# Retention in a hybrid encoder layer: the second half's sums of squares in their own stretch, operand splits moved up and down

## The chip, the cores and the metric

The kernel runs on one core of one Trainium2 chip. The core has a matrix engine (TensorE, PE in the profile), VectorE (DVE), ScalarE (ACT), GpSimd (POOL) and a queue engine, SyncE (SP), that issues most of the DMAs. The metric is the device time of one execution in microseconds (us).

## The reference, cut to what matters

One encoder layer over 1024 tokens of width 1024, in float32:

```python
u = x @ w_in                                    # one projection for both groups of heads
y_ret = GroupNorm(ret_fwd + ret_bwd) * gn_gain * silu(gate)   # 8 heads of 64, chunks of 128
y_att = windowed_gqa(aq, ak, av, sink)          # 8 heads of 64, window +-128
mix   = concat(y_ret, y_att) @ w_out
h     = LN1(alpha * x + mix)
f     = (silu(h @ w_ffn_gate) * (h @ w_ffn_up)) @ w_ffn_down \
        + sigmoid(h @ w_ple_gate) * (p @ w_ple_proj)
out   = LN2(alpha * h + f)
```

GroupNorm runs over the 64 elements of a head: mean, then `rsqrt(mean of squares + eps)`. The change concerns where the sums of squares of this GroupNorm are made, and when some weights are prepared that later stages use.

## The kernel before, in words

**Numbers.** Each float32 product is made of three fast matmuls. An operand is split into a rounded part (hi) and a remainder (lo), and hi x hi, hi x lo and lo x hi are added up in PSUM (`mm3`, lines 77 to 79; in the output projection and later `mm3c`, lines 803 to 805). A split is a copy on ScalarE and a subtraction on VectorE.

**Stages.** After the first projections, the retention heads and attention heads are worked through in four pairs (`NPAIR`): pair i has two retention heads and two attention heads. Around them, further projections of `x` (queries, keys, the gates) run as filling: `enqueue` cuts them into 16 steps a tile (three matmuls of 512 columns each step), and `take` runs so many of these steps at a time. One step of the filling is one *tick*. `run(steps, total)` executes a hand-written list; at each `F` in it, it takes its share of `total` ticks. There is a *stretch* of 48 ticks for the retention of pair 0, one each for pairs 1, 2 and 3 (which hold that pair's attention too), and a last `run` of 16 ticks. These I call stretch 0, 1, 2, 3 and the last run.

**In a stretch** the list has, for the retention, `K` (keys turned and decayed), `r.kv`, `Q` (scores), `r.scan`, `Y` (outputs of a half of the tokens), `E` (`evict`: squares of the half, their split into hi and lo, a copy of the half), `M` (`norm`), and for the attention `sco`, `trn`, `val`. Halves are numbered 0 and 1. `M(h)` multiplies the split squares by a matrix of ones (line 498), so the sums stand in PSUM, and VectorE turns them into a row (line 500). The rest is put into `later`, with due times in ticks after `M` (`LAGS = (3, 6, 9, 12, 15)`): `spread` sends the row to a small tile by DMA (line 505), `power` takes the inverse root on GpSimd (line 508), `store` writes it to DRAM (line 511), `fetch` reads it back over all partitions (line 515), `scaled` multiplies the half by it (line 519). Later the gate of the pair multiplies it too (lines 722 to 724).

**Side work.** Weights that the next stages need as split sums are prepared in the same stretches. Each piece is a `put` (lines 602 to 604): ScalarE copies hi, VectorE subtracts, and SP writes both to DRAM; some puts add or subtract two blocks first (lines 638 and 663). `presplit_out(kt, ...)` makes seven such pieces of the output weights (`wod`), `presplit_small(n, ...)` two pieces of the small operands (`ptd` for n 0 and 1, `ped` for n 2 and 3), `presplit_gate()` 28 pieces of the embedding gate's weights (`pgd`), spread over stretches 0 and 1. All have due times in ticks in the list `side`. The buffers of a put: two in turn for the gate; one (`op`) for all puts of stretch 2, and one for all of stretch 3.

**Order.** In these stretches TensorE's order is the order of the program (`manual_schedule(engines={PE})`). A planner orders the other engines by its own costs; `behind` only tells it that an operation comes after the latest projection matmul. Each engine then executes its list in order, with semaphores for what it depends on. At the end `bp.close()` frees the tiles of the stretches, and the output projection (`product`, lines 825 to 839) begins. Its right operands come from `wod` in DRAM through `stream` (line 814), into tiles of two kinds, `w` and `u`, in turn; `u` lies where tiles of the stretches lay. From there SP's own order is the program's as well.

Of the kernel before, what the change touches and what calls it, by code (L numbers as in the profile page):

```python
# [10 lines left out]
F32R = mybir.dt.float32r  # L11
# [5 lines left out]
P = 128  # L17
S = 1024
# [3 lines left out]
HF = 512  # L22
# [20 lines left out]
def layer(tc, xT, xn, w_first, w_mt, w_rv, w_out, w_pg, w_pe, pT, w_gu, w_dn,  # L43
# [53 lines left out]
    def rawt(w):  # L97
        return wp.tile([P, w], F32, tag="raw", bufs=2, name=nm("raw"))
# [34 lines left out]
    def bt(shape, tag, bufs=None, dt=F32):  # L133
        return bpool.tile(list(shape), dt, tag=tag, bufs=bufs, name=nm(tag))
# [15 lines left out]
    with tc.manual_schedule(engines={mybir.EngineType.DVE, mybir.EngineType.SP}):  # L150
        for kt in range(KT):
            r = xraw[kt]
# [128 lines left out]
    later, side, ticks = [], [], [0]  # L281
# [314 lines left out]
    ped = dr.tile([2, 2, P, 2, HF], F32, name="ped")  # L596
    ptd = dr.tile([4, P, 2, HF], F32, name="ptd")
# [3 lines left out]
    def put(x, o, dst):  # L601
        behind(act.activation(o[:, 0, :], x, AF.Copy))
        behind(dve.tensor_tensor(o[:, 1, :], x, o[:, 0, :].bitcast(F32), ALU.subtract))
        sp.dma_start(dst, o.bitcast(F32))

    def presplit_small(n, o, start):

        hold = []

        def load():  # L610
            r = rawt(2 * HF)
            hold.append(r)
            if n < 2:
                for j in range(4):
                    sp.dma_start(r[:, j * 2 * P:(j + 1) * 2 * P], pT[4 * n + j])
            else:
                sp.dma_start(r, w_pe[n - 2])

        def step(j):
            put(hold[0][:, j * HF:(j + 1) * HF], o, ptd[2 * n + j] if n < 2 else ped[n - 2, j])  # L620

        return [(ticks[0] + start + at, f) for at, f in ((0, load), (4, lambda: step(0)), (7.5, lambda: step(1)))]

# [21 lines left out]
    def presplit_gate():  # L645

        first, other = ([a_tile([P, 2, HF], "pre", t) for _ in range(2)] for t in ("A1", "A0"))
        ops = [a_tile([P, 2, HF], "pro", "A1", F32R) for _ in range(2)]
        n = [0]

        def load(k):
            for j in range(2):
                sp.dma_start((other if k == 1 else first)[j], w_pg[j, k])

        def steps(k):
            raw = other if k == 1 else first

            (a11, a21), (a12, a22) = ([raw[j][:, i, :] for i in range(2)] for j in range(2))

            def s(p, x, *sums):  # L660
                def f():
                    for a in sums:
                        behind(dve.tensor_tensor(*a))
                    put(x, ops[n[0] % 2], pgd[p - 1, k])
                    n[0] += 1
                return f

            return [s(1, a11), s(4, a22), s(2, a12), s(5, a22, (a22, a21, a22, ALU.add)),
                    s(7, a21, (a21, a11, a21, ALU.subtract)), s(6, a11, (a11, a22, a11, ALU.subtract)),
                    s(3, a12, (a12, a12, a11, ALU.subtract))]  # L670

        load(0)
        load(1)
        k0, k1, k2, k3 = map(steps, range(4))
        k1[0] = pair_of(k1[0], lambda: load(2))
        k3[0:0] = [lambda: load(3), lambda: None]
        at = [2 + 3.4 * k for k in range(12)] + [55 + 2.5 * k for k in range(2)] + [60 + 2.2 * k for k in range(7)] + \
            [75 + 2.3 * k for k in range(9)]
        return [(ticks[0] + t, f) for t, f in zip(at, k0 + k1 + k2 + k3, strict=True)]

    def pair_of(f, g):
# [58 lines left out]
    with tc.manual_schedule(engines={mybir.EngineType.PE}):  # L740
        enqueue([mtile(0, ev_av), proj_rv(), *project(1), *project(2), *project(3), gate(0), gate(1), gate(2), gate(3)])

        spare.append(bt([P, S], "aq", 3, F32R))
        twin = lambda t: t.rearrange("p (a b) -> p a b", a=2)
        ops = [twin(spare[1]), a_tile([P, 2, HF], "pro", "A0", F32R)]
        side.extend(presplit_out(0, ops, 17.5, 4))
        side.extend(presplit_out(1, ops, 44, 4, spare[:1]))
        a = Attention(0, ytile(1))
        sco, trn, val = (lambda n: (a.scores, n)), (lambda n: (a.turn, n)), (lambda n: (a.values, n))
        run([F, F, sco(0), F, sco(1), F], 16)  # L750
        run([F, (av_turn, 0), (av_turn, 1), F, trn(0), sco(2), F, trn(1), sco(3), F, val(0), val(1), trn(2), sco(4), F,
             trn(3), sco(5), F, val(2), val(3), trn(4), sco(6), F, trn(5), sco(7), F, val(4), val(5), trn(6), (decay_q, 0),
             F, trn(7), (decay_k, 0, 0), F, val(6), val(7), (decay_k, 0, 1), F], 64)
        assert not side and not later
        y0 = ytile(0)
        side.extend(presplit_gate())
        states = state_tile()
        r = Retention(0, y0, states)
        K, M = (lambda q: (r.keys, q)), (lambda q: (r.norm, q))
        Q = lambda q: (r.scores, q)  # L760
        Y, E = (lambda q: (r.out, q)), (lambda q: (r.evict, q))
        run([K(0), F, K(1), F, F, (r.kv,), Q(0), F, (r.scan,), F, F, F, Y(0), E(0), Q(1),
             F, M(0), (decay_q, 1), F, (decay_k, 1, 0), Y(1), E(1), (decay_k, 1, 1), F, F], 48)
        V = []
        for i in range(1, NPAIR):
            assert i == 1 or not side, len(side)
            M1 = M(1)
            r = Retention(i, ytile(2 * i), states)
            a = Attention(i, ytile(2 * i + 1))
            if i == 2:  # L770
                late = [ytile(6), ytile(7)]
                op = twin(late[1].bitcast(F32R))
                side.extend(presplit_out(2, [op], 2, 3.5, late[:1]))
                side.extend(presplit_small(0, op, 30) + presplit_small(1, op, 38))
            elif i == 3:
                op = twin(bt([P, S], "aq", 3, F32R))
                side.extend(presplit_out(3, [op], 4, 3.5, [bt([P, S], "rk", 2)]))
                side.extend(presplit_small(2, op, 32) + presplit_small(3, op, 40))
            G = [(f, i + 1, *x) for f, x in ((decay_q, ()), (decay_k, (0,)), (decay_k, (1,)))] if i + 1 < NPAIR else \
                [(lambda: None,)] * 3  # L780
            run([K(0), M1, F, K(1), sco(0), F, *V, (r.kv,), Q(0), F, sco(1), F, trn(0), sco(2), (r.scan,), F, trn(1),
                 sco(3), F, val(0), val(1), F, trn(2), sco(4), F, trn(3), sco(5), F,
                 Y(0), E(0), val(2), val(3), Q(1), F, G[0], trn(4), sco(6), M(0), F, G[1], trn(5), sco(7), F,
                 G[2], Y(1), val(4), val(5), E(1), F, trn(6), F, trn(7), F], 48)
            V = [val(6), val(7)]
        run([*V, M(1), F, F, F], 16)

    bp.close()

# [1183 lines left out]
```

## Time and profile before

| | us |
|---|---|
| median of 3 runs (lowest, highest) | 1177.18 (1176.48, 1179.31) |
| the profiled execution | 1177.34 |
| its span, first to last instruction | 1174.9 |
| TensorE busy | 1157.9 (99%) |
| VectorE busy | 900.5 (77%) |
| ScalarE busy | 580.6 (49%) |
| GpSimd busy | 120.1 (10%) |

The granted clock of TensorE is 0.998 of full speed over the span. Times in the rows below are microseconds from the start of the span. By TensorE's timeline, stretch 1 runs from 163.9 to 223.2, stretch 2 to 283.9, stretch 3 to 343.5, the last run to 356.2, where the output projection begins. A row of a timeline gives start, duration, engine, line, operation, the tiles written and read (without their numbers), and in brackets the idle time of the engine before it and what ended it. A trailing "q" on an engine's name is its instruction queue, where DMAs are issued. In a row of waits stand the engine and line that waited, what it waited for, total us, times and the longest one.

### The profile page before, as it was taken

To read this page: it belongs to the slowest core of one execution; us is meant where nothing else is said; L and a number is where in the kernel's file an instruction comes from. 1 tells how busy PE (TensorE), PEld (TensorE's weight loads), DVE (VectorE), ACT (ScalarE), POOL (GpSimd) and SP (SyncE) were. 2 spreads that over 40 slices of the span, in tenths; PEclk is the share of its full clock that TensorE was granted. 3 is DMA by queue.
4 is the path that set the end of the run, shared out by engine and by line. 5 is a ranking of instruction groups with operands and counts; after the bars stand their busy time and mean duration, and the time that the engine had idled before them with its cause. 6 is when DMAs were issued, how large, how long until landed. Compare 5 with 4: busy or idle time off the path is not lost.

```text
span 1174.9 us, 17927 instructions
## 1 busy us (share of the span) xinstructions
PE 1157.9 (99%) x6330; PEld 971.8 (83%) x6330; DVE 900.5 (77%) x1746; ACT 580.6 (49%) x1181; POOL 120.1 (10%) x181
## 2 busy tenths in 40 slices
PE   9999999999998999999999999999999999999996
PEld 7888888888886888887888888888888888888885
DVE  4666688777859688947998988888888875774677
ACT  5566348676756266213444434443344445552463
POOL 2001020202010031000000000000000011133232
PEclk9999999999999999999999999999999999999999
DMA  6345666646446945756322322333224289999977
GB/s 251 94 157 206 244 206 229 216 146 209 154 153 227 384 162 186 286 180 214 114 75 101 132 100 82 125 123 112 99 72 135 80 250 340 350 233 204 261 173 215
DMA packets 84377, 213.86 MB, mean 182 GB/s; under 512 B 12224, under 2 KB 17472, under 8 KB 84288
## 3 DMA queue, kind: packets, MB, share of 16 engines
q1 hardware_dynamic: 75648, 195.94, 47.0%
q0 software_dynamic: 8640, 16.78, 8.2%
q8 instruction: 50, 0.82, 0.3%
q14 instruction: 39, 0.32, 0.1%
HBM read 141.32 MB, written 62.16 MB: 173 GB/s over the span
## 4 chain that ended last, share of the span: by engine, by line
PE 81%; DVE 7%; ACT 5%; DMA 4%; issue 2%; SPq 0%; POOL 0%; DVEq 0%; ACTq 0%; POOLq 0%
PE bmm L803 8%; PE bmm L804 7%; PE bmm L805 7%; PE bt L803 6%; PE bt L804 6%; PE bt L805 6%; PE bs L805 4%; PE bs L804 4%; PE bs L803 4%; PE bo L805 3%; PE bo L803 3%; PE bo L804 3%; PE bmm L77 3%; PE bmm L78 3%; PE bmm L79 3%
## 5 line engine op out<-in xcount | busy, mean ns | idle before, releaser
L77 PE MATMUL bmm<-H,w 128*128 128x512 f32 x240 | 96.9, 404 | 0.0
L78 PE MATMUL bmm<-H,w 128*128 128x512 f32 x240 | 94.1, 392 | 0.0
L79 PE MATMUL bmm<-H,w 128*128 128x512 f32 x240 | 93.8, 391 | 0.0
L1388 ACT ACTIVATE ev<-ev 128x512 f32<-128x512 f32 x42 | 26.5, 630 | 104.3 <-DVE ev L1417 92.8
L1562 POOL DMA_DIRECT2D h0b<-in_w_dn x24 | 21.6, 902 | 541.2 <-DVE ev L1368 505.5
L77 PEld LDWEIGHTS bmm<-H,w 128*128 128x128 f32 x240 | 45.1, 188 | 11.2 <-issue 1.2
L79 PEld LDWEIGHTS bmm<-H,w 128*128 128x128 f32 x240 | 45.2, 188 | 10.3
L78 PEld LDWEIGHTS bmm<-H,w 128*128 128x128 f32 x240 | 45.3, 189 | 8.1
L554 ACT ACTIVATE sc<-sc,st 128x385 f32<-128x385 f32 (+1 forms) x64 | 37.2, 584 | 15.6 <-DVE st L552 15.4
L550 DVE CUSTOM_DVE_ANT_0 sc<-cst,bs,skb 128x384 f32<-128x384 f32 (+1 forms) x64 | 34.8, 574 | 9.3 <-PE bs L549 8.6
L1417 DVE TENSOR_TENSOR ev<-ev,bt 128x512 f32<-128x512 f32 x44 | 30.1, 683 | 12.5 <-PE bt L805 12.5
L1368 DVE TENSOR_TENSOR ev<-ev,bs 128x256 f32<-128x256 f32 x63 | 25.6, 418 | 15.5 <-PE bs L805 14.7
L1390 DVE TENSOR_TENSOR ev<-ev 128x512 f32<-128x512 f32 x42 | 29.0, 691 | 10.5 <-ACT ev L1388 9.0
L803 PE MATMUL bmm<-H,u 128*128 128x512 f32 x92 | 36.2, 393 | 0.2 <-ACT ev L1426 0.2
L804 PE MATMUL bmm<-H,u 128*128 128x512 f32 x92 | 36.1, 392 | 0.0
L805 PE MATMUL bmm<-H,u 128*128 128x512 f32 x92 | 35.8, 389 | 0.0
L560 ACT ACTIVATE sc<-sc,st 128x384 f32<-128x384 f32 (+1 forms) x64 | 34.1, 580 | 0.6 <-DVE st L558 0.5
L71 ACT ACTIVATE H<-ln 128x512 fp32r<-128x512 f32 (+1 forms) x34 | 22.7, 676 | 23.0 <-DVE ln L1052 7.2
L545 POOL COPY sc<-skb 128x1 f32<-128x1 f32 x64 | 15.5, 252 | 180.6 <-PE bt L572 141.9
L72 DVE TENSOR_TENSOR w<-raw,w 128x512 fp32r<-128x512 f32 x34 | 23.1, 686 | 13.8 <-ACT w L71 13.7
L803 PE MATMUL bmm<-H,w 128*128 128x512 f32 x84 | 32.9, 392 | 0.0
L804 PE MATMUL bmm<-H,w 128*128 128x512 f32 x84 | 32.9, 392 | 0.0
(800 smaller groups left out, 3897.8 us busy)
## 6 DMA issues: line engine op xcount, KB each, us to landing
ad<-ev SPq DMA_DIRECT2D x33, 512.0 KB, 2.6
pgd<-pro SPq DMA_DIRECT2D x28, 512.0 KB, 2.9
raw<-in_w_gu SPq DMA_DIRECT2D x22, 512.0 KB, 3.6
ln<-in_w_gu SPq DMA_DIRECT2D x22, 512.0 KB, 4.1
raw<-ad SPq DMA_DIRECT2D x40, 256.0 KB, 5.9
ln<-ad SPq DMA_DIRECT2D x37, 256.0 KB, 6.6
H<-in_w_dn SPq DMA_DIRECT2D x33, 256.0 KB, 7.6
wod<-aq SPq DMA_DIRECT2D x15, 512.0 KB, 2.8
```

The source lines that it names most:

```text
L77: pe.matmul(o, lh, rh, start=start, stop=False)
L78: pe.matmul(o, lh, rl, start=False, stop=False)
L79: recent[0] = pe.matmul(o, ll, rh, start=False, stop=stop).ins.name
L550: dve.tensor_tensor_reduce(sc[g][:, :nk], cst[:, tc0:tc0 + nk], b[:, :nk], slope(i, g), skb[:, 2 * i + g:2 * i + g + 1], ALU.add, ALU.max, ...
L554: act.activation(sc[g][:, :nk + 1], sc[g][:, :nk + 1], AF.Exp, bias=st_[:, 1, j, g:g + 1], accum_out=st_[:, 2, j, g:g + 1])
L560: behind(act.activation(sc[g][:, :nk], sc[g][:, :nk], AF.Copy, scale=st_[:, 3, j, g:g + 1]))
L803: pe.matmul(o, lh, rh, start=start, stop=False, skip_group_check=True)
L804: pe.matmul(o, lh, rl, start=False, stop=False, skip_group_check=True)
L805: pe.matmul(o, ll, rh, start=False, stop=stop, skip_group_check=True)
L1388: act.activation(c[:, 0, :], c[:, 0, :], AF.Silu)
L1390: dve.tensor_tensor(c[:, 1, :], c[:, 0, :], c[:, 1, :], ALU.mult)
L1417: dve.tensor_tensor(get(name), ev[left][:, m, :], right, ALU.add)
```

## The change

- `M(1)`, the sums of squares of the second half, moves from the next stretch (after its `K(0)`; for pair 3, the last run) into its own: at the end of stretch 0, and ahead of `trn(7)` in stretches 1 to 3. The due times of its `spread` to `scaled` are counted from there.
- In stretch 3, the gap between the output weights' puts goes from 3.5 to 3.1 ticks, and the small operands start at ticks 27 and 34 in place of 32 and 40. The last of them is loaded into the tile that held a raw output weight (`rkx`), and its first put uses a second buffer, in the other tile of the tag `rk`.
- In stretch 1, the gate's third group of puts starts at tick 65 in place of 60, 1.9 ticks apart in place of 2.2; the fourth at 78.5 in place of 75, 2 apart in place of 2.3. (These ticks count from the start of stretch 0; its last put is due at 94.5 in place of 93.4.)

```diff
-    def presplit_small(n, o, start):
+    def presplit_small(n, o, start, raw=None, other=None):
...
-            r = rawt(2 * HF)
+            r = rawt(2 * HF) if raw is None else raw
...
-            put(hold[0][:, j * HF:(j + 1) * HF], o, ptd[2 * n + j] if n < 2 else ped[n - 2, j])
+            put(hold[0][:, j * HF:(j + 1) * HF], o if j or other is None else other(), ptd[2 * n + j] if n < 2 else ped[n - 2, j])
...
-        at = [2 + 3.4 * k for k in range(12)] + [55 + 2.5 * k for k in range(2)] + [60 + 2.2 * k for k in range(7)] + \
-            [75 + 2.3 * k for k in range(9)]
+        at = [2 + 3.4 * k for k in range(12)] + [55 + 2.5 * k for k in range(2)] + [65 + 1.9 * k for k in range(7)] + \
+            [78.5 + 2 * k for k in range(9)]
...
         run([K(0), F, K(1), F, F, (r.kv,), Q(0), F, (r.scan,), F, F, F, Y(0), E(0), Q(1),
-             F, M(0), (decay_q, 1), F, (decay_k, 1, 0), Y(1), E(1), (decay_k, 1, 1), F, F], 48)
+             F, M(0), (decay_q, 1), F, (decay_k, 1, 0), Y(1), E(1), (decay_k, 1, 1), F, F, M(1)], 48)
...
-            M1 = M(1)
...
-                side.extend(presplit_out(3, [op], 4, 3.5, [bt([P, S], "rk", 2)]))
-                side.extend(presplit_small(2, op, 32) + presplit_small(3, op, 40))
+                rkx = bt([P, S], "rk", 2)
+                side.extend(presplit_out(3, [op], 4, 3.1, [rkx]))
+                side.extend(presplit_small(2, op, 27) + presplit_small(3, op, 34, rkx, lambda: twin(bt([P, S], "rk", 2, F32R))))
...
-            run([K(0), M1, F, K(1), sco(0), F, *V, (r.kv,), Q(0), F, sco(1), F, trn(0), sco(2), (r.scan,), F, trn(1),
+            run([K(0), F, K(1), sco(0), F, *V, (r.kv,), Q(0), F, sco(1), F, trn(0), sco(2), (r.scan,), F, trn(1),
                  sco(3), F, val(0), val(1), F, trn(2), sco(4), F, trn(3), sco(5), F,
                  Y(0), E(0), val(2), val(3), Q(1), F, G[0], trn(4), sco(6), M(0), F, G[1], trn(5), sco(7), F,
-                 G[2], Y(1), val(4), val(5), E(1), F, trn(6), F, trn(7), F], 48)
+                 G[2], Y(1), val(4), val(5), E(1), F, trn(6), F, M(1), trn(7), F], 48)
             V = [val(6), val(7)]
-        run([*V, M(1), F, F, F], 16)
+        run([*V, F, F, F], 16)
```

## The prediction

> **What bounds the kernel now.** I read the page first, then the list of who waited for whom on TensorE, then that engine's timeline where the longest wait stands, and from there the queue that released it.
>
> ```profile
> span 1174.9 us, 17927 instructions
> ...
> PE 1157.9 (99%) x6330; PEld 971.8 (83%) x6330; DVE 900.5 (77%) x1746; ACT 580.6 (49%) x1181; POOL 120.1 (10%) x181
> ```
>
> TensorE (PE) is busy for nearly all of the span. The change adds no matmul and takes none away, so it can only move the time by adding or removing moments in which PE waits. PE's own waits are few:
>
> ```profile
> PE bt L803 <- DMA u<-wod: 3.2, 2, 2.9
> ...
> PE bt L77 <- DVE sg L1098: 0.9, 1, 0.9
> PE bt L572 <- ACT ptr L574: 0.8, 1, 0.8
> PE bt L428 <- DVE pt L411: 0.7, 1, 0.7
> PE bt L572 <- ACT sc L560: 0.4, 1, 0.4
> ```
>
> Columns: total us, times, longest. The first is the largest by far: the output projection's first product waits for operands that were split earlier, written to DRAM (`wod`) and are now fetched. The L77 wait lies far behind the changed code. The other three lie inside the retention and attention stretches that the change rearranges. PE's timeline at the first wait:
>
> ```profile
> 356.22 0.39 PE L803 MATMUL bt<-w,H 128*128 128x512 f32 x1
> ...
> 359.98 0.47 PE L803 MATMUL bt<-u,H 128*128 128x512 f32 x1 [2.92 <-DMA u<-wod]
> ...
> 361.21 0.47 PE L803 MATMUL bt<-w,H 128*128 128x512 f32 x1 [0.30 <-DMA w<-wod]
> ...
> 362.46 0.47 PE L803 MATMUL bt<-u,H 128*128 128x512 f32 x1 [0.31 <-DMA u<-wod]
> ...
> 363.22 0.40 PE L803 MATMUL bt<-w,H 128*128 128x512 f32 x1
> ...
> 365.96 0.39 PE L803 MATMUL bs<-w,H 128*128 128x512 f32 x1
> ```
>
> Each L803 opens a group of three matmuls on one of four operands. The second column of the product (363.22 to 365.96) takes 2.74 us for its four groups. The first column, from 356.22 to 363.22, takes 7.00. So the waits with their restarts cost 7.00 - 2.74 = 4.26 us. Why the operands were late is on SyncE's queue (SP), which issues in order:
>
> ```profile
> 348.04 1.12 SPq L505 DMA_DIRECT2D sn<-kv  x2
> 352.37 0.33 SPq L511 DMA_DIRECT2D rnd<-sn  x1
> 353.12 0.33 SPq L604 DMA_DIRECT2D ped<-aq  x1
> 353.81 1.10 SPq L515 DMA_DIRECT2D rb<-rnd  x2
> 354.96 0.58 SPq L814 DMA_DIRECT2D u<-wod  x1
> 355.58 0.43 SPq L814 DMA_DIRECT2D w<-wod  x1
> 356.06 0.43 SPq L814 DMA_DIRECT2D u<-wod  x1
> ```
>
> The three operand loads (L814) stand directly behind the last pair's normalisation: spread the row of sums (L505), store the inverse roots (L511), fetch them back (L515). Between the first two, GpSimd takes the power. One split of the last small operand (`ped`, L604) stands there as well. What starts this chain is the second half's sum of squares, `M(1)`, which before is in the stretch after its own:
>
> ```profile
> 340.20 0.60 PE L572 MATMUL bt<-cst,sc 128*128 128x128 f32 x4
> 344.75 0.50 PE L498 MATMUL bo<-pt,ones 128*128 128x512 f32 x1
> 345.08 0.40 PE L498 MATMUL bo<-rb,ones 128*128 128x512 f32 x1
> 341.83 0.69 DVE L603 TENSOR_TENSOR aq<-raw,aq 128x512 fp32r<-128x512 f32 x1 [2.83 <-ACT aq L602]
> 347.34 0.67 DVE L500 TENSOR_SCALAR kv<-bo 2x512 f32<-2x512 f32 x1
> 350.50 1.84 POOL L508 TENSOR_TENSOR sn<-sn,cst 128x8 f32<-128x8 f32 x1 [17.46 <-DMA sn<-kv]
> ```
>
> **M(1) in its own stretch.** In the last stretch it goes ahead of `trn(7)`, the L572 at 340.20, so it issues there and not at 344.75. Its two matmuls keep their length (start 0.33 apart, the last 0.40 long), so the sums stand at about 340.9 where they stood at 345.48. VectorE then makes the row (L500). Before, that came 347.34 - 345.48 = 1.86 us later. It could also be at once, since VectorE sat idle for 2.83 us ahead of 341.83. Row start: 340.9 to 342.8. From the row's start to the first operand load the queue took 354.96 - 347.34 = 7.62 us: the row, two transfers to their landing, 1.84 of power, the issue of the fetch. GpSimd was idle, so nothing stretches that. The first load then issues at 348.5 to 350.4; I take 349.5, between two ends that decide the same. The other two follow 0.62 and 1.10 later, as now.
>
> From issue to use the three took 359.98 - 354.96 = 5.0, 361.21 - 355.58 = 5.6 and 362.46 - 356.06 = 6.4 us. At the later end they arrive at 355.4, 356.6 and 357.9. Unhindered, PE wants them one, two and three quarters of 2.74 us behind 356.22, at 356.9, 357.6 and 358.3. All three are in time, so the full 4.26 us goes. Next late would be the left operands, which are other tiles and held PE nowhere in the first column of the product; behind that, the last window quoted further down, where PE was never idle.
>
> The Trainium skill (DMA: Bandwidth & Descriptors, Anatomy of one DMA) fits a transfer at about 2.0 us plus its bytes over 436 GB/s, an estimated 3.2 us for these 512 KB; by that PE would have waited for the first operand alone and the removal would be worth about 1.3 us. The rows above show 5.0 to 6.4 us for these loads, so the measured 4.26 stands, and the fit gets no chance of its own.
>
> PE gains no work from the move: the same two matmuls in another place. What it may add is a wait for the squares' remainder (L491), because M(1) comes earlier. The tightest place is stretch 1:
>
> ```profile
> 217.89 0.68 DVE L491 TENSOR_TENSOR rb<-qq,pt 128x512 fp32r<-128x512 f32 x1
> 220.03 0.60 PE L572 MATMUL bt<-cst,sc 128*128 128x128 f32 x4
> 223.92 0.39 PE L498 MATMUL bo<-rb,ones 128*128 128x512 f32 x1
> 229.41 0.68 DVE L500 TENSOR_SCALAR kv<-bo 2x512 f32<-2x512 f32 x1
> ```
>
> The remainder is done at 218.57 and M(1) would start at 220.03: 1.46 us to spare, cost 0. If VectorE's order slips by more than that, M(1), `trn(7)` and the projection matmuls behind them wait on PE; three stretches that each slip by twice that margin would cost 3 x 1.46 = 4.4. The other way, the row at 229.41 leaves VectorE's crowded start of stretch 2, where the 0.7 us wait for L411 is: gain 0 to 0.7.
>
> **The splits moved up, with a second buffer.** A split is a ScalarE copy (L602), a VectorE subtraction (L603) and a write on SP (L604). All those of stretch 3 used one buffer, so each waits for the write before it:
>
> ```profile
> 323.65 0.63 ACT L602 ACTIVATE aq<-rk 128x512 fp32r<-128x512 f32 x1 [1.15 <-DMA wod<-aq]
> ...
> 328.08 0.63 ACT L602 ACTIVATE aq<-rk 128x512 fp32r<-128x512 f32 x1 [1.67 <-DMA wod<-aq]
> ...
> 341.16 0.63 ACT L602 ACTIVATE aq<-raw 128x512 fp32r<-128x512 f32 x1 [2.31 <-DMA ped<-aq]
> ...
> wod<-aq SPq DMA_DIRECT2D x15, 512.0 KB, 2.8
> ```
>
> How long the stretches are and how busy the engines in them:
>
> ```profile
> 163.90:223.20 59.30, 58.48 (x453) 48.90 (x452) 48.74 (x120) 43.90 (x106) 9.14 (x22) 1.00 0.58 202
> 283.90:343.50 59.60, 59.21 (x473) 49.43 (x471) 46.28 (x115) 39.82 (x95) 7.11 (x14) 1.00 0.43 151
> 367.00:420.00 53.00, 53.00 (x240) 43.97 (x239) 43.23 (x77) 21.89 (x48) 4.53 (x3) 1.00 0.80 296
> ```
>
> The columns are the length, then the busy time of PE, PE's loads, VectorE, ScalarE and GpSimd. One buffer's round is 0.63 + 0.69 + 0.33 + 2.8 = 4.45 us. Stretch 3 has 48 ticks in 59.6 us, 1.24 each, so the old gap of 3.5 ticks is 4.35 us and the new one of 3.1 is 3.85. Each round is then 0.6 us short of its buffer, and over some eight rounds ScalarE stands still for about 4.8 us in front of a split, with its exponentials and evictions queued behind, for which PE's transposes wait. Bounds on PE: 0 and 4.8. I take 0: the waits of 1.15 and 1.67 above are of that kind and the whole stretch cost PE 0.39 us idle (59.60 - 59.21), and ScalarE is busy for 39.82 of 59.60. What it buys is that the last `ped` write leaves SP's queue: the last split is due at tick 41.5, about 335.4, and even 4.8 us late it is written more than 8 us before 349.5. The new load of that operand's raw half reuses a buffer that the output splits read last at tick 27.6, and is issued at tick 34; six ticks (7.5 us) cover it, and without them SP would hold back the weights of the last gate behind it. Cost 0.
>
> **The gate's splits moved down.** They use two buffers in turn, so a gap of 1.9 ticks of 59.3/48 = 1.24 us is 4.7 us per buffer, over the 4.45 of a round: no new shortfall. They start 5 ticks (6.2 us) later, which clears the place where PE waited 0.8 for a ScalarE eviction: gain 0 to 0.8. They end 1.1 ticks later, so the next stretch's load into the same tiles is up to 1.4 us later, with ticks of cover before its first split: 0.
>
> **Sum.** 4.26 gained at the output projection; the small gains (0 to 1.5) I set against new waits of the same kind, at 0. The profiled execution is 1177.34 us (a span of 1174.9 and 2.4 around it), 0.16 over the median, so it stands for the median: 1177.2 - 4.3 = 1172.9 us.
>
> **Rivals.** (a) The chain isn't shortened as much, because the row is left waiting on VectorE, whose order a planner chooses and not the program. In stretch 1 the row started 229.41 - 224.31 = 5.1 us after its sums. With that delay here the row starts at 346.0, the load at 353.6, 1.4 us earlier than now: 1175.8. For it speaks that delay; against it that VectorE is idle here. (b) The gain is given back in stretch 3: ScalarE's 4.8 us reach PE in full, 1172.9 + 4.8 = 1177.7. (c) Slower: the split at the head of ScalarE's queue waits longer than reckoned, 1.7 us at each (the mean of the three waits quoted), for the ten splits of stretch 3, 17 us in all. Where about 10 of those reach PE the time is 1172.9 + 10 = 1183; it decides above 7.8 us, which is the gain of 4.26 and 0.3% on top. Against it: those same three waits reached PE with at most 0.4. The Trainium skill (TensorE: Matmul & The Clock Gate, Architectural detail) says that the queues of ScalarE and VectorE are strictly first in, first out; the rows' idle ScalarE in front of a split agrees, and it is the rule that speaks against packing them closer.
>
> **Chances.** Forecast 0.60, (a) 0.15, (b) 0.12, (c) 0.13. About 0.3% (3.5 us) is what a measurement of this kernel can tell from no change. The forecast lies beyond it, (a) and (b) within: faster 0.60, same 0.27, slower 0.13. The range runs from the forecast with all small gains, 1172.9 - 1.5 = 1171.4, to (b), 1177.7; only (c) is left out.
>
> **What would show it.** Right: no L803 wait for `wod` at the start of the product, the first `u<-wod` issued near 349.5, M(1) near 340, the row within 2 us of it, no `ped` write behind 345. Wrong: PE waits for L491 at M(1), or new PE waits for ScalarE (L574, L560) in stretches 1 and 3 that sum to several us, or a later wait of the product on another operand.

## The result, and the profile after

The changed kernel takes 1171.12 us (median of 5 runs, 1170.19 to 1172.70) against 1177.18 (5 runs, 1175.41 to 1179.31): a ratio of 0.9948 with a 95% interval of 0.9931 to 0.9964. By this interval it is faster by more than 0.3%. Timed twice more beside the kernel before, its medians were 1171.27 and 1170.99, with ratios of 0.9955 and 0.9961 and intervals that reach to 0.9967 and 0.9975. The forecast was 1172.9, its range 1171.4 to 1177.7: the direction is right, the median lies 0.3 us below the range. The profiled execution is 1172.70 us, the longest of its five.

Busy times on the page of after, and TensorE's list of waits:

```profile
span 1170.6 us, 17933 instructions
...
PE 1156.5 (99%) x6330; PEld 971.5 (83%) x6330; DVE 900.4 (77%) x1746; ACT 580.1 (50%) x1181; POOL 121.0 (10%) x181
```

```profile
PE bt L428 <- DVE pt L411: 2.0, 1, 2.0
...
PE bs L803 <- ACT h0b L972: 0.6, 1, 0.6
PE bt L803 <- DMA u<-wod: 0.4, 1, 0.4
PE bt L77 <- DMA p<-ptd: 0.3, 1, 0.3
PE bt L572 <- ACT ptr L574: 0.3, 1, 0.3
```

The wait for `wod` fell from 3.2 us to 0.4. A wait that was not there before has come in, of the same line for a ScalarE eviction (L972), and the wait for L411 rose from 0.7 to 2.0. PE's timeline of after, with M(1), the first column of the first product (354.63 to 358.36) and the place of the new wait:

```profile
338.60 0.40 PE L498 MATMUL bo<-pt,ones 128*128 128x512 f32 x1
338.83 0.40 PE L498 MATMUL bo<-rb,ones 128*128 128x512 f32 x1
...
354.63 0.39 PE L803 MATMUL bt<-w,H 128*128 128x512 f32 x1
...
357.58 0.48 PE L803 MATMUL bt<-u,H 128*128 128x512 f32 x1 [0.38 <-DMA u<-wod]
...
358.36 0.39 PE L803 MATMUL bt<-w,H 128*128 128x512 f32 x1
...
371.68 0.39 PE L803 MATMUL bt<-u,H 128*128 128x512 f32 x1
...
373.07 0.50 PE L803 MATMUL bs<-w,H 128*128 128x512 f32 x1 [0.55 <-ACT h0b L972]
```

The first column takes 3.73 us where it took 7.00. SP's queue of after:

```profile
338.79 0.33 SPq L814 DMA_DIRECT2D w<-wod  x1
339.56 0.33 SPq L604 DMA_DIRECT2D ped<-aq  x1
340.15 1.40 SPq L505 DMA_DIRECT2D sn<-kv  x2
347.05 0.33 SPq L511 DMA_DIRECT2D rnd<-sn  x1
347.47 0.38 SPq L604 DMA_DIRECT2D ped<-aq  x1
348.49 1.11 SPq L515 DMA_DIRECT2D rb<-rnd  x2
349.65 0.58 SPq L814 DMA_DIRECT2D u<-wod  x1
350.32 0.38 SPq L814 DMA_DIRECT2D w<-wod  x1
350.74 0.43 SPq L814 DMA_DIRECT2D u<-wod  x1
```

The first load is issued 354.63 - 349.65 = 4.98 us ahead of the product; before it was 356.22 - 354.96 = 1.26. The row that starts the chain (VectorE), the power (GpSimd), and stretch 3 in the list of windows:

```profile
339.45 0.67 DVE L500 TENSOR_SCALAR kv<-bo 2x512 f32<-2x512 f32 x1
```

```profile
345.38 1.64 POOL L508 TENSOR_TENSOR sn<-sn,cst 128x8 f32<-128x8 f32 x1 [12.16 <-DMA sn<-kv]
```

```profile
284.00:343.60 59.60, 59.60 (x488) 50.03 (x486) 46.93 (x116) 39.39 (x96) 6.89 (x14) 1.00 0.50 170
```

PE was idle for 0.39 us in this stretch before and is not idle in it now.

**Where the time went.** I cut PE's matmul timeline at the starts of the first filling matmul (L77) of each stretch and at matmuls of the output projection: its first product has 16 groups of L803 to L805, four of them the first column, and the second product 16 more. After minus before, in us: up to stretch 1, 162.81 - 163.47 = -0.66; stretches 1 to 3, 179.50 - 180.54 = -1.04; last run, 11.02 - 10.90 = +0.12; first column -3.28; rest of the first product -0.02; second product, 12.13 - 10.88 = **+1.25**; all behind it, 782.72 - 783.40 = -0.68. The sum is -4.31; the profiled executions differ by 1172.70 - 1177.34 = -4.64.

### The profile page after: what moved, and what is told of

It reads as the page before. It is cut to its first block, busy times and chain, and to the rows that moved or that the text cites. A ratio compares the mean times of both kernels' runs of the same rounds, so it can differ in the third digit from the quotient of the medians.

```text
span 1170.6 us, 17933 instructions
## 1 busy us (share of the span) xinstructions
PE 1156.5 (99%) x6330; PEld 971.5 (83%) x6330; DVE 900.4 (77%) x1746; ACT 580.1 (50%) x1181; POOL 121.0 (10%) x181
## 4 chain that ended last, share of the span: by engine, by line
PE 86%; DVE 6%; DMA 4%; ACT 2%; issue 1%; POOL 0%; SPq 0%; DVEq 0%; ACTq 0%; POOLq 0%
PE bmm L803 8%; PE bmm L804 8%; PE bmm L805 7%; PE bt L803 6%; PE bt L804 6%; PE bt L805 6%; PE bmm L77 4%; PE bs L803 4%; PE bs L805 4%; PE bs L804 4%; PE bmm L79 4%; PE bmm L78 4%; PE bo L805 3%; PE bo L803 3%; PE bo L804 3%
## 5 line engine op out<-in xcount | busy, mean ns | idle before, releaser
L77 PE MATMUL bmm<-H,w 128*128 128x512 f32 x240 | 97.3, 405 | 0.0
L77 PEld LDWEIGHTS bmm<-H,w 128*128 128x128 f32 x240 | 45.1, 188 | 11.1 <-issue 1.4
L803 PE MATMUL bmm<-H,u 128*128 128x512 f32 x92 | 36.2, 393 | 0.2 <-ACT ev L1426 0.2
L805 PE MATMUL bmm<-H,u 128*128 128x512 f32 x92 | 35.8, 389 | 0.0
L560 ACT ACTIVATE sc<-sc,st 128x384 f32<-128x384 f32 (+1 forms) x64 | 34.2, 580 | 1.2 <-DVE st L558 0.9
L71 ACT ACTIVATE H<-ln 128x512 fp32r<-128x512 f32 (+1 forms) x34 | 22.7, 675 | 21.2 <-DVE ln L1052 7.2
L803 PE MATMUL bmm<-H,w 128*128 128x512 f32 x84 | 32.9, 392 | 0.0
```

Source lines behind the costliest of these rows:

```text
L77: pe.matmul(o, lh, rh, start=start, stop=False)
L560: behind(act.activation(sc[g][:, :nk], sc[g][:, :nk], AF.Copy, scale=st_[:, 3, j, g:g + 1]))
L803: pe.matmul(o, lh, rh, start=start, stop=False, skip_group_check=True)
L805: pe.matmul(o, ll, rh, start=False, stop=stop, skip_group_check=True)
```

## The experiments

Each was timed in 5 rounds beside the kernel before. The kernels e1 to e3 and e8 were timed together, then e5, e6, e9 and e10, then e12 to e15, then e16 to e18; before took 1176.07, 1177.10, 1176.88 and 1176.58 in these four groups. The last three columns are cut from PE's timeline as above, of the one profiled execution of each kernel.

| kernel | what it is | us | ratio, 95% | stretches 1 to 3 | first column | second product |
|---|---|---|---|---|---|---|
| before | | 1177.18 | 1 | 180.54 | 7.00 | 10.88 |
| e1_m1 | M(1) alone | 1172.93 | 0.9969, 0.9957 to 0.9981 | 179.39 | 5.94 | 10.88 |
| e2_splits | splits alone | 1172.44 | 0.9970, 0.9958 to 0.9982 | 180.94 | 4.76 | 10.88 |
| e3_gate | gate alone | 1175.99 | 0.9997, 0.9987 to 1.0007 | 180.08 | 6.33 | 10.88 |
| e5_last_splits | splits, last pair's M(1) | 1173.99 | 0.9973, 0.9964 to 0.9983 | 181.38 | 3.74 | 12.20 |
| e6_m1_splits | splits, M(1) | 1173.08 | 0.9962, 0.9949 to 0.9975 | 178.61 | 2.72 | 12.21 |
| e17_nogate | the same again | 1172.76 | 0.9964, 0.9952 to 0.9977 | 179.75 | 2.72 | 12.19 |
| after | all three | 1171.12 | 0.9948, 0.9931 to 0.9964 | 179.50 | 3.72 | 12.13 |
| e8_after | after again | 1171.27 | 0.9955, 0.9943 to 0.9967 | 179.63 | 3.06 | 12.15 |
| e16_after | after again | 1170.99 | 0.9961, 0.9947 to 0.9975 | 179.05 | 2.72 | 12.20 |
| e9_order | after, evictions ahead | 1171.01 | 0.9946, 0.9934 to 0.9959 | 178.91 | 2.72 | 10.88 |
| e15_order | the same again | 1170.00 | 0.9946, 0.9933 to 0.9958 | 178.95 | 3.43 | 11.16 |
| e14_order_ng | e6, evictions ahead | 1169.57 | 0.9941, 0.9929 to 0.9954 | 178.12 | 2.74 | 11.35 |
| e18_order_ng | the same again | 1170.78 | 0.9945, 0.9929 to 0.9961 | 179.37 | 2.72 | 11.36 |
| e13_first | after, last pair's M(1) late | 1171.49 | 0.9955, 0.9941 to 0.9968 | 180.09 | 5.24 | 10.88 |
| e12_chain | after, chains of pairs 1, 2 late | 1171.91 | 0.9957, 0.9944 to 0.9969 | 180.59 | 2.72 | 11.44 |
| e10_pool | after, last chain on GpSimd's queue | 1178.96 | 1.0021, 1.0009 to 1.0033 | 178.45 | 11.69 | 12.00 |

**One part at a time.** e1_m1 is before with only the M(1) lines of the diff:

```diff
-F, F], 48)                    # stretch 0
+F, F, M(1)], 48)
-run([K(0), M1, F, K(1), ... trn(6), F, trn(7), F], 48)
+run([K(0), F, K(1), ... trn(6), F, M(1), trn(7), F], 48)
-run([*V, M(1), F, F, F], 16)
+run([*V, F, F, F], 16)
```

> The kernel before with M(1) alone moved into its own stretch; splits and gate as before. Theory A (SyncE's order at the output projection: the first operand load stands behind both the last fetch and the last ped write, so M(1) and the splits pay only together): the chain is shorter, but the last ped write, whose split ScalarE reached at 349.5, keeps the load near 353.5; the first column of the first product loses about 2.9 us instead of 4.3. Time 1175.5 to 1176.5, 1 to 2 us faster. Theory B (M(1) pays by itself, in every stretch): 1171 to 1173. Theory C (any rearrangement shuffles the planner's order and the time moves by chance): no pattern, anything from 1172 to 1180, with new TensorE waits in the stretches.

e2_splits is before with only the splits:

```diff
-side.extend(presplit_out(3, [op], 4, 3.5, [bt([P, S], "rk", 2)]))
-side.extend(presplit_small(2, op, 32) + presplit_small(3, op, 40))
+rkx = bt([P, S], "rk", 2)
+side.extend(presplit_out(3, [op], 4, 3.1, [rkx]))
+side.extend(presplit_small(2, op, 27) + presplit_small(3, op, 34, rkx, lambda: twin(bt([P, S], "rk", 2, F32R))))
```

> The kernel before with the splits of stretch 3 alone moved up, second buffer included; M(1) and the gate as before. Theory A: the fetch of the last normalisation still ends at about 355, the load behind it too; the wait at the product stays at about 3 us, time within 1 us of 1177.2. Theory B: no gain either, 1177. Rival D (ScalarE and SyncE held by the splits were the cause, not M(1)): 1172 to 1174.

e3_gate is before with only the gate's due times:

```diff
-[60 + 2.2 * k for k in range(7)] + [75 + 2.3 * k for k in range(9)]
+[65 + 1.9 * k for k in range(7)] + [78.5 + 2 * k for k in range(9)]
```

> The kernel before with the gate's puts alone moved down. Theory A: the product's wait is unchanged; the 0.8 us wait of TensorE for a ScalarE eviction at 183 falls to about 0.3, so 0.3 to 0.8 us faster: 1176.4 to 1176.9, hardly measurable. Rival E (the gate's move carries the missing 1.8 us of gain): 1175.4 or less.

M(1) alone and the splits alone are each worth about 0.3%, by different ways. The rows of e2 (PE, VectorE, SP; its L815 is the load):

```profile
345.47 0.40 PE L498 MATMUL bo<-rb,ones 128*128 128x512 f32 x1
```

```profile
345.96 0.67 DVE L500 TENSOR_SCALAR kv<-bo 2x512 f32<-2x512 f32 x1
```

```profile
353.42 0.58 SPq L815 DMA_DIRECT2D u<-wod  x1
```

In e2 the row is made 345.96 - 345.87 = 0.09 us after its sums, where it was 1.86. Before, a split's subtraction (L603) stood ahead of it on VectorE, waiting for its copy on ScalarE (L602), which waited for a write of `ped`; of before:

```profile
345.46 0.63 ACT L602 ACTIVATE aq<-raw 128x512 fp32r<-128x512 f32 x1 [1.25 <-DMA ped<-aq]
346.13 0.69 DVE L603 TENSOR_TENSOR aq<-raw,aq 128x512 fp32r<-128x512 f32 x1 [1.20 <-ACT aq L602]
```

With the splits out of the way the chain starts on time, and the load goes 1.54 us earlier without M(1) having moved. In e1 the row is early, but the last write of `ped` is still there, right ahead of the load (SP of e1; L813 is the load):

```profile
347.21 1.10 SPq L515 DMA_DIRECT2D rb<-rnd  x2
350.67 0.33 SPq L604 DMA_DIRECT2D ped<-aq  x1
351.03 0.43 SPq L813 DMA_DIRECT2D u<-wod  x1
```

The load goes 3.93 us earlier than before, but the product begins 2.13 earlier too (354.09), and the first column keeps 5.94. (The list of waits of e1 puts the longest one there to ScalarE's split of `h`, a tile that the waiting matmul, `bt<-u,H`, doesn't read; the load of `u` landed at 356.58, and the matmul started at 356.72.) In the first column M(1) gains 1.06, the splits 2.24, all three parts together (after and its repeats) 3.28 to 4.28. In e1 the first column explains only a third of what the whole kernel gained, 1176.07 - 1172.93 = 3.14.

The gate's move shows nothing in the time (0.9997). Its 6.33 in the first column lies far from its own edit, and I have no cause for it.

**The parts together.** e6_m1_splits leaves the gate's due times as before; e8_after is the changed kernel again:

```diff
-[65 + 1.9 * k for k in range(7)] + [78.5 + 2 * k for k in range(9)]
+[60 + 2.2 * k for k in range(7)] + [75 + 2.3 * k for k in range(9)]
```

> The changed kernel with the gate's puts left where they were before: M(1) and the splits moved. Theory H (the gain lies at the output projection: M(1) takes about 1.1 us off the first column of the first product, the splits about 2.2, both 3.3 to 3.9, and 1.25 comes back at the second product, where TensorE waits for ScalarE's evictions; the gate's move is worth 0 to 1 us in stretch 1): 1171.2 to 1172.2, a first column of 3 to 3.7 us, a second product of 12.1. Rival I (the gate's move matters once the rest is done): 1173 or more.

> The changed kernel once more, for a second profile and a second set of times. Theory F (the two profiled executions differ by 4.3 us of span, as forecast, and the 6.1 us between the medians holds some spread of the executions): the ratio comes nearer to 0.996, 4.5 to 5.5 us faster, and the spans of one kernel differ by 1 to 3 us in places that the change does not touch (the first loads, the last stores). Rival G (the change really gains 6 us and the profiled execution was a slow one): 0.9948 again, and a profile whose span is 1168 to 1169, shorter than the first one's in places behind the output projection.

e5_last_splits has the splits, and of M(1) only that of the last pair:

```diff
-trn(6), F, trn(7), F], 48)
+trn(6), F, *([M(1)] if i == NPAIR - 1 else []), trn(7), F], 48)
-run([*V, M(1), F, F, F], 16)
+run([*V, F, F, F], 16)
```

> The kernel before with M(1) of the last pair alone in its own stretch, and the splits moved; M(1) of pairs 0 to 2 and the gate as before. Theory H: the output projection is as in the changed kernel, since it knows the last pair alone: first column 3 to 3.7 us, second product 12.1, time 1171.2 to 1172.5. Rival J (M(1) of the earlier pairs gives a good part, in stretches 1 and 2): 1173 or more, stretches 1 and 2 together over 1 us longer than in the kernel with all M(1) moved.

The last pair's M(1) is the only one whose chain stands ahead of the projection's loads. It takes another 1.0 us off the first column (4.76 in e2, 3.74 in e5), and the second product grows by 1.3. The total is no better than the splits alone (0.9973 against 0.9970). That points to a new bound in the second product, and to gains from the other pairs' M(1) that the forecast had put at nothing.

**The new bound in the second product.** The timelines say what it is. Of before, on PE, ScalarE and VectorE:

```profile
376.84 0.39 PE L803 MATMUL bs<-w,H 128*128 128x512 f32 x1
```

```profile
375.25 0.58 ACT L972 ACTIVATE h0b<-bs 128x512 f32<-128x512 f32 x1
```

```profile
374.00 0.68 DVE L876 TENSOR_TENSOR ln<-ln,y 128x512 f32<-128x512 f32 x1
```

and of after, ScalarE and VectorE:

```profile
371.90 0.63 ACT L71 ACTIVATE h0a<-ln 128x512 fp32r<-128x512 f32 x1 [1.78 <-DVE ln L876]
372.44 0.58 ACT L972 ACTIVATE h0b<-bs 128x512 f32<-128x512 f32 x1
```

```profile
371.19 0.68 DVE L876 TENSOR_TENSOR ln<-ln,y 128x512 f32<-128x512 f32 x1
```

PE would be at this group at 371.68 + 0.68 = 372.36, which is 4.48 us earlier than before (376.84). The eviction (L972) that frees its accumulator comes only 2.81 us earlier. ScalarE has the finished accumulator at hand, but in its list a split of a left operand (L71) stands ahead, and waits for VectorE's sum (L876). VectorE runs through those sums and splits without a pause, and as a whole it moved up by 2.81. Before, the eviction was done 376.84 - 375.83 = 1.0 us ahead of PE; now it is done at 373.02, 0.7 too late. With the restart behind it this makes 0.83 of the 1.25; most of the rest is lost at the group of 369.51, to the eviction before it. Where the first column has lost its waits altogether, the second product's first group is late too: in e16, e6 and e17 it starts 0.94, 1.21 and 1.45 us behind the group ahead of it, in place of 0.68, and e6's and e17's lists of waits name the same line, L972, for it (0.4 and 0.6 us). The column "second product" begins at that group and doesn't show this. The Trainium skill (TensorE: Matmul & The Clock Gate, Architectural detail) calls the queues of ScalarE and VectorE strictly first in, first out; these rows agree.

If that is so, an eviction that doesn't stand behind those splits takes the wait away. e9_order puts the last three splits of that operand behind the last eviction; e15 is e9 again, e14 and e18 are the same edit with the gate as before.

```diff
-        halfop(s4o, kt, yx[kt])
+        if kt == 0:
+            halfop(s4o, kt, yx[kt])
...
-        act.activation(s1[k], X[k], AF.Copy)
+        ev = act.activation(s1[k], X[k], AF.Copy)
+    for kt in range(1, 4):        # the same split, ordered behind ev
+        ...
```

> The changed kernel with ScalarE's four evictions of the first product put ahead of the last three splits of the fifth operand, which wait for VectorE. Theory H: the second product falls from 12.1 to about 11.0 us and the time by about 1.1, to 1170.1. Rival K (the operands themselves, made by VectorE, have become the bound): the second product gets shorter but the third waits as much longer; time 1171.2 as before.

> The changed kernel with the evictions put ahead, a second time, to see whether it beats the changed kernel: if the 1.25 us of the second product count to the end, 1169.5 to 1170.3 and a ratio of 0.9940 or less; if later stages take them back, 1171 and 0.995.

> M(1) and splits moved, the gate's puts where they were before, and ScalarE's four evictions of the first product ahead of the operand splits that wait for VectorE. Theory H2: stretches 178.4 to 179.6 (without the gate's move stretch 1 is 0.7 longer and stretch 2 about 1 shorter), first column 2.7 to 3.7, second product 10.9, time 0 to 1.5 us below the version without that order. Rival (the gate's move is worth 1 us or more in the time): 1171.5 or more.

> The same with ScalarE's four evictions of the first product ahead of the waiting operand splits. If that gain reaches the end: 1 to 1.5 us below both, ratio to before 0.9935 to 0.9945; if later stages take it back, the same as the kernel without the order.

ScalarE and PE of e9 (L973 is the eviction):

```profile
367.35 0.63 ACT L71 ACTIVATE H<-ln 128x512 fp32r<-128x512 f32 x1
367.88 1.07 ACT L973 ACTIVATE h0b<-bs 128x512 f32<-128x512 f32 x2
```

```profile
370.19 0.39 PE L803 MATMUL bs<-w,H 128*128 128x512 f32 x1
```

The evictions are done at 368.95, the group runs at 370.19 without a wait, and the second product is back at 10.88 in e9. In the other three it is 11.16 to 11.36, most of the way (the earlier eviction keeps its place in the edit). So the mechanism of the second product's loss is shown. What the edit is worth in the whole kernel is not resolved: e9 and e15 have 0.9946, the changed kernel 0.9948, and 0.9955 and 0.9961 in its repeats, with intervals that overlap. The lowest ratios of all are those of e14 and e18, with 0.9941 and 0.9945; they beat before, and are not set apart from the changed kernel.

**M(1) of the earlier pairs.** e13_first leaves the last pair's M(1) where it was; e12_chain puts M(1) early on PE, but in pairs 1 and 2 makes the row, and all that hangs on it, as late as before.

```diff
 # e13
-F, M(1), trn(7), F], 48)
+F, *([M(1)] if i < NPAIR - 1 else []), trn(7), F], 48)
-run([*V, F, F, F], 16)
+run([*V, M(1), F, F, F], 16)
 # e12
+home, wait = rnd[2 * self.i + hh], 4 if hh and self.i in (1, 2) else 0
+if wait:
+    later.append((ticks[0] + wait + 1, make_row))
+else:
+    make_row()
...
-later.extend((ticks[0] + at, f) for at, f in ...)
+later.extend((ticks[0] + wait + at, f) for at, f in ...)
```

> The changed kernel with M(1) of the last pair left in the last run, those of pairs 0 to 2 moved, splits and gate moved. Theory H2 (the output projection gains 2.2 us by the splits; M(1) of the last pair adds 1 us there, which the second product gives back; the rest of the gain is in the stretches): stretches 178.4 to 179.6, first column 4.8, second product 10.9, time within 0.7 us of the changed kernel. Rival (my first account: M(1) of the last pair is the main part): 1173 or more.

> The changed kernel, where M(1) of pairs 1 and 2 keeps its early place on TensorE, but its row on VectorE and the transfers behind it are due where they were before, at the start of the next stretch. In the profiles so far, stretches 1 to 3 take 178.4 to 179.6 us with all M(1) moved and 180.1 to 181.4 with those of pairs 1 and 2 where they were. Theory P (the row and its chain leave the crowded start of stretches 2 and 3, which is what gains there): the three stretches return to 180 or more, time 1 to 1.7 us above the changed kernel. Theory Q (what gains is M(1)'s place on TensorE, since the buffers that it reads come free earlier): 178.4 to 179.6 as before, time as the changed kernel's.

e13 is as fast as after: with the last pair's M(1) early, the first column goes from 5.24 to 3.72 or less, and the second product gives 1.25 back. For the earlier pairs the single stretches say more than their sum. Stretch 3 lasts 60.46 to 61.17 us in the four kernels in which M(1) of pairs 1 and 2 is late, and 60.03 to 60.35 in the thirteen in which it is early: 0.7 us between the means, with no overlap. In stretch 2 it is 60.70 to 61.53 (three kernels) against 59.49 to 60.21 (five) with the gate's splits as before, 1.3 us between the means. With the gate's splits moved it is 60.78 (one) against 60.23 to 61.24 (seven, without e12): nothing. In stretch 3 most of it lies in one wait: 18 to 19 us into the stretch, PE waits for ScalarE's L560 for 0.4 to 1.0 us in the four kernels, and for 0.2 at most in the thirteen.

e12 asks whether it is the time of the chain that counts. Its rows come 7.3 and 5.1 us into stretches 2 and 3, later than before's 5.3 and 4.0. Its stretch 2 lasts 62.29, 1.6 more than the mean of those seven (60.69), but PE was not held up longer there: its wait for L411 is 1.94 us, and 1.97 in after. Behind that wait the granted clock fell to half for 3.4 us. The windows of e12 (the granted clock is the third number from the end):

```profile
232.90:236.30 3.40, 3.40 (x19) 2.79 (x18) 2.64 (x7) 3.01 (x9) 1.65 (x1) 0.50 0.48 154
```

PE's matmuls in it start 0.43 us apart in place of 0.23. At half the clock 3.4 us hold 1.7 us of work, and without the other 1.7 this stretch would be at 60.6, by estimate, among the seven. Why the clock fell here, and not behind the same wait in after, is not shown. Stretch 3 keeps the gain (60.09) with its chain late. So nothing here speaks for the time of the chain. What the thirteen share is M(1)'s early place on PE; how that lets ScalarE reach L560 in time stays open.

**The gate again.** e16_after and e17_nogate (the code of e6) ran side by side to see what the gate's move is worth.

> The changed kernel, for comparison on one chip with the next two: ratio 0.995, some 1171 us, stretches 1 to 3 179.5, first column 3 to 3.7, second product 12.1.

> M(1) and the splits moved, the gate's puts where they were before. If the gate's move is worth nothing, within 0.7 us of the changed kernel, stretch 1 about 0.4 longer and stretch 2 about 1.1 shorter; if it is part of the gain, 1.5 us or more above it.

The ratios are 0.9961 and 0.9964, with one interval nearly upon the other; the medians are 1170.99 and 1172.76, from 9 and 10 runs that spread over 5.3 and 5.5 us. A gain of up to a microsecond or two is not excluded. In the traces the move takes 0.7 us off stretch 1 (means: 59.04 in eight kernels without it, 58.36 in nine with it) and, with M(1) early, adds 0.8 to stretch 2 (59.86 to 60.69). In stretch 1 the wait for ScalarE's L574 is 0.6 to 0.8 us without the move and 0.3 or less with it; in stretch 2 PE waits longer for L411: 1.4 to 2.0 in all nine kernels with the gate's move, and 0.8 or less in the eight without it.

**The chain on another queue.** e10_pool issues the last pair's spread, store and fetch from GpSimd, so that the operand loads do not stand behind them at all.

```diff
+q = pool if self.i == NPAIR - 1 and hh else sp
...
-sp.dma_start(home, sm[:, 1])
+q.dma_start(home, sm[:, 1])
```

> The changed kernel with the three transfers of the last pair's second normalisation issued by GpSimd in place of SyncE, so that the first operand loads stand behind the last ped write alone. Theory H: they issue at about 348 in place of 350, the first column falls to 2.74 us (0.3 to 1.0 less), and the second product takes the gain back, since ScalarE's evictions there stand behind VectorE's operands: 1170.7 to 1171.3. Rival L (the loads themselves are slow, whenever they issue): the first column stays at 3 to 3.7 us. Rival M (slower transfers from GpSimd make the last half late, and the left operands of the third product with it): 1172 or more.

It is slower than before. GpSimd, VectorE and PE's wait in e10 (L517 is the fetch, L521 the half's multiplication, L807 PE's line):

```profile
346.94 0.62 POOL L513 DMA_DIRECT2D rnd<-sn  x1 [0.29 <-POOL sn L510]
353.15 1.04 POOL L517 DMA_DIRECT2D rb<-rnd  x2 [5.59 <-PE bmm L79]
```

```profile
360.31 0.75 DVE L521 SCALAR_TENSOR_TENSOR y<-y,gn,rb 128x512 f32<-128x512 f32 x1 [9.47 <-DMA rb<-rnd]
360.97 3.70 DVE L72 TENSOR_TENSOR H<-y,H 128x512 fp32r<-128x512 f32 x6
```

```profile
PE bt L807 <- DVE H L72: 7.1, 1, 7.1
```

The first operand load went out at 346.35, 3.3 us earlier than in after, and it was no use. The fetch was issued 4.7 us later than in after and landed 6.4 us after its issue. The row names PE as what ended GpSimd's wait in front of it; the store that the fetch reads landed 5.7 us after its issue at 346.94, so at about 352.6, which fits better. VectorE stood 9.47 us in front of L521 with the six splits of PE's left operands behind it. Behind that wait the granted clock was at half, and PE was busy for 3.49 us of this stretch, which costs another 1.7 by estimate:

```profile
358.40:365.20 6.80, 3.49 (x8) 2.81 (x9) 4.89 (x9) 0.00 (x0) 0.00 (x0) 0.50 0.34 119
```

So the chain has two ends at the projection: the right operands, through SP's order, and the left ones, through VectorE's. The forecast had seen the first one only.

## Why the prediction was right or wrong, point by point

- **M(1) near 340, the row within 2 us:** right. M(1) at 338.60, the row at 339.45, 0.22 after the end of the sums.
- **The first load at 349.5:** 349.65, but by two errors that cancel. From the row to the load I took 7.62 us; it was 349.65 - 339.45 = 10.20. The spread's small transfer was ready for GpSimd 345.38 - 341.55 = 3.8 us after the end of its issue, where it was 350.50 - 349.16 = 1.3: in after, two transfers of 512 KB had been issued 1.4 and 0.6 us ahead of it. The earlier row made up for it, so that the number came out is luck.
- **No write of `ped` behind 345:** wrong, there is one at 347.47. Its copy on ScalarE started at 344.97, 9.6 us behind the 335.4 that the forecast gave, and the list names the `ped` write ahead of it (issued at 339.56), which shares its buffer. It stands ahead of the fetch, where SP waited anyway.
- **The full 4.26 us of the first column:** 3.28 in the profiled execution, 3.94 and 4.28 in the repeats. The forecast left the start of the product at 356.22, 6.7 us behind the first load. The stretches ahead of it got shorter, it began at 354.63, and the lead was 4.98. Also the third operand came 357.58 - 350.74 = 6.84 us after its issue, where the forecast reckoned with 6.4. In before's rows the three waiting groups start 1.23 and 1.25 us apart though their loads were issued 0.62 and 0.48 apart: 512 KB in 1.24 us, some 420 GB/s. So the 5.0, 5.6 and 6.4 us hold the time behind the load ahead, and it is the lead of the first that matters. The Trainium skill's fit (DMA: Bandwidth & Descriptors, Anatomy of one DMA), which that section gives for DMAs on GpSimd's path, would by its 3.2 us have had 1.3 gained; 3.28 and more speaks against using it for these loads from SyncE's queue.
- **"Next late would be the left operands ... PE was never idle":** this step failed. The second product gave 1.25 us back, by ScalarE's evictions behind splits that wait for VectorE. The forecast had read the window behind the product as free, since PE did not wait there before; the margin of 1.0 us in it was to be read from the eviction's end and the next use of its accumulator. With the late first group of the second product, the net gain at the output projection is 2.0 to 2.7 in place of 4.26. From its start to the end of the second product it takes 26.06 us in before, 24.01, 23.41 and 23.34 in the three executions of after, and 23.81 and 24.29 in e2 and e13, which leave the last pair's M(1) late: the move that the forecast put first adds nothing clear there.
- **"The small gains I set against new waits, at 0":** this step failed too. With M(1) early, stretches 1 to 3 sum to 178.1 to 179.8 in the ten kernels that have it in all pairs with the chain on SP and in time, 180.1 to 181.4 in the four that have it late. That is about 1.6 us between the means (179.1 and 180.7), where the forecast allowed 1.5 at most and took 0. In the profiled pair it is 1.04.
- **The sum:** the two failed terms nearly cancel. 2.0 to 2.7 at the projection and about 1.6 in the stretches make 3.6 to 4.3 us, so the forecast's 4.3 was near by luck. They don't explain a median below the range: it shows 6.1 us, the repeats 4.8 and 5.6, which lie inside the 5.8 that the range allowed. The cause of what goes beyond 4.3 stays open.
- **M(1)'s margin over L491, the density of the splits, rivals (b) and (c):** the costs of 0 were right. There is no wait for L491, and stretch 3, where ScalarE was to stand still, has no idle PE at all.
- **Rival (a), the row left waiting on VectorE:** the reverse holds. It had waited before, behind a split, and the splits' move alone sets it free (e2). The idle VectorE ahead of 341.83, which the forecast read as room for the row, was of the same kind: a split at the head of its list, waiting for ScalarE.
- **The gate, 0 (0 to 0.8):** right within what was measured.

**What stays open.** First column, second product and stretches make 3.28 - 1.25 + 1.04 = 3.07 us; the profiled executions differ by 4.64, the medians by 4.8 to 6.1. Of the rest, 0.66 lies ahead of stretch 1, 0.58 of it in the first nine microseconds of the kernel (last section). Another 0.68 lies behind the second product, most of it around 530 us, where PE waits in L77 (0.93 in before, for VectorE's L1098; 0.31, 0.57 and none in the three executions of after, for the load from `ptd`). Between two executions of one and the same kernel this part differed by up to 1.8 us (e9 and e15), so I don't put it down to the change.

## What to carry to other kernels

When a wait of the busiest engine is taken away, go along the next places where it meets the engines that don't move up with it, and read the margin there (the end of the release against the start of the use), not only whether there was a wait. Before a longer stretch is put down to a wait, look at the clock that was granted in it. A long chain of small transfers hurts all that stands behind it in each in-order queue it passes through, the issuing queue and the engines that consume its result alike, and what delays it may be a piece of unrelated side work at the head of one of these. Small terms that look like noise, several of them of one sign, can be as large as what is given back at the main term.

## What the runs showed of the hardware that was not expected

**The start of the kernel is not the same from run to run.** PE's timeline at the beginning, before and after:

```profile
5.92 0.63 PE L77 MATMUL bt<-H,w 128*128 128x512 f32 x1
6.34 0.63 PE L77 MATMUL bo<-H,w 128*128 128x512 f32 x1
6.77 0.53 PE L78 MATMUL bmm<-H,w 128*128 128x512 f32 x1
```

```profile
5.87 0.41 PE L77 MATMUL bt<-H,w 128*128 128x512 f32 x1
6.12 0.39 PE L77 MATMUL bo<-H,w 128*128 128x512 f32 x1
6.35 0.39 PE L78 MATMUL bmm<-H,w 128*128 128x512 f32 x1
```

The matmuls start 0.43 us apart until 6.8 us in before, and 0.23 apart from 5.9 us on in after; in e1 they are at 0.23 from 5.2 us on. The trace's records of the granted clock have full speed from 7.06 us on in before, from 5.87 in after and from 4.46 in e1. The first 48 ticks take 32.8 to 33.9 us accordingly. The Trainium skill (TensorE: Matmul & The Clock Gate, What's actually happening) says that the array runs at half its clock until a window of activity of some 3.4 us, which runs free of the kernel's start, has been busy; the two paces and the varying moment agree with it, and so do the half-clock stretches inside e12 and e10, of 3.4 and 6.8 us. In the seventeen profiled executions the four kernels with M(1) late all have a long start (163.17 to 163.47 us up to stretch 1), those with it early 162.37 to 163.25. Of the 0.66 between before and after, 0.58 has built up by 9 us. Nothing that the change moves lies in these, and why it falls out so was not settled.

**The spread landed late behind large transfers, whichever queue issued it.** In e10 the last fetch of 128 KB took 6.4 us to land and the store of 4 KB 5.7, from GpSimd's queue, with operand loads of 512 KB issued just ahead of both. From SP's queue the same two took 4.3 and 1.4 in before, and 3.7 and 1.4 in after; nothing had been issued on SP's queue in the 3 us ahead of that store. The spread tells queue and company apart: in after (SP) and in e10 (GpSimd) it goes out behind the same two transfers of 512 KB, issued 0.6 to 1.8 us ahead. The `--dma` view of 338 to 346 us, of after and of e10 (KB each, median us to landing):

```profile
sn<-kv SPq DMA_DIRECT2D x2, 2.0 KB, 4.7
```

```profile
sn<-kv POOLq DMA_DIRECT2D x2, 2.0 KB, 4.4
```

In before, with none of them on their way, the spread was ready 1.3 us after the end of its issue. So for the spread it was the company that mattered, not the queue. The store and the fetch of e10 can be read the same way, but no run has them on GpSimd's queue without the loads.
